# Up-projection of a decoder step: the four sums of weight blocks of a feature pair made by adding transfers instead of vector adds, their signs turned, and the weights fetched one more pair ahead

## The chip, the cores and the metric

The kernel runs on one core of a Trainium2 chip. The metric is the device time of one execution in microseconds, the median of several. A profile of one further execution gives the busy time of each engine and a trace of its instructions. The engines are TensorE (PE; its weight loads are listed as PEld), VectorE (DVE), ScalarE (ACT), GpSimd (POOL) and SyncE (SP), which only issues transfers. Each engine runs its own list of instructions in order. Transfers run on 16 DMA engines; SyncE, ScalarE and GpSimd issue them from their lists.

## The reference

One step of a decoder layer for 1024 prompt rows and 8 sequences of 4 sample rows, 1056 rows in all. The change lies in the feed-forward part:

```python
h2 = rmsnorm(x, g_norm2) * (1 + scale2) + shift2
up = h2 @ w_up                       # 1056 x 1024 by 1024 x 5632
prev = zeros if conv_prev is None else conv_prev
upc = concatenate([prev, up], axis=1)
conv = b_conv
for k in range(CONV_W):              # causal, depthwise, width 3
    conv = conv + w_conv[k] * upc[:, k:k + T]
a, gv = split(conv, 2, axis=-1)      # 2816 features each
x = x + gate2 * ((gelu(a) * gv) @ w_down)
```

Before it stand the norms, a gated chunk mixer, the attention with its page gathers, and `w_out`; behind it the final norm. All is float32.

## The kernel before

Features stand on the 128 partitions and rows run along the free dimension. `x1`, `hr` and the results are tiles of 128 x 1056 for 128 features each (R = 1056; HR = 528 is half of the rows; HB = 264 a quarter, which is what one PSUM bank takes in a matmul here). A float32 product is made in three matmuls per 128 x 128 block. Both operands are split into a leading part and a remainder (for weights by `parts`: ScalarE's cast L328, VectorE's subtraction L329), and the products leading x leading, leading x remainder and remainder x leading are summed in PSUM (L61).

The up-projection runs over 22 *pairs* of feature blocks: pair j makes block j of the `a` half (tile `ua`) and block 22 + j of the gate half (tile `ug`). It treats the product as a 2 x 2 block product: the weights of a pair are four blocks of 128 x 512, `a11`, `a12` (block j, input features 0 to 511 and 512 to 1023) and `a21`, `a22` (block 22 + j), and the activations four of 512 x 528. Seven products of blocks are then enough rather than eight. Four of them have sums of weight blocks as their weights:

```python
s1 = a21 + a22;  s2 = s1 - a11;  s3 = a11 - a21;  s4 = a12 - s2
```

and four have sums of activation blocks, `T1` to `T4`, which are made once. `F[k]`, `b1(k)`, `b2(k)` and `sums_of` are steps on the way to them, `turned` splits one of them into its two parts, and `B22` is the split block of the last activations. One `product` is 4 blocks of 128 inputs x 3 matmuls x 2 banks = 24 matmuls of 264 columns.

`pair_weights(j)` issues the loads of the four blocks on SyncE (`raw_load`, L1402, a ring of six tiles `raw`), loads the sample rows' convolution state `cst` (L1576), and makes the sums in two large tiles (`add_up`, L1582 to L1585), on GpSimd for every pair but the first and on VectorE for pair 0. It is called for pair j just ahead of `pair(j, ...)`. The large tiles come from `slot()`, a ring shared with the activation tiles, so a new pair waits until an old tile is free.

For pairs 0 to 3, `first_products` has the two products with `a11` and `a12` begun while the last rows of the activations are still in the making, between the steps of their norm: the squares of the last eighth (ScalarE L1463) are added (VectorE L1464), summed over the features on TensorE, and turned into scales. The other five products of these pairs follow later, in `pair`. In it VectorE adds the products into `ua` and `ug` (L1604, L1647), ScalarE copies (L1635), and `conv` makes the convolution of either half in three steps (ScalarE L1555, VectorE L1556 and L1557), with two small copies of the last rows on GpSimd (L1551, L1552). Then come gelu on ScalarE (L1660), the product of the halves on GpSimd (L1661, L1663), and the store of the result (L1664, GpSimd's queue). A new `up` tile begins with a memset on GpSimd (L1532) and the state rows (L1596).

The list of each engine is fixed when the program is built: a scheduler places the instructions of the program there, not always in the order of the source, and a position once given is kept whatever the chip then does.

## Time and profile before

| | |
|---|---|
| median of 3 runs | 1919.66 us (1917.22 to 1921.19) |
| the profiled execution | 1922.04 us, its span 1920.4 us |
| mean granted TensorE clock | 0.99 |
| first 264-column matmul of the up-projection | 1173.48 us |
| end of its last one | 1647.55 us |
| 264-column matmuls in between | 3696 |
| moved over the span | 345.09 MB, 180 GB/s |

Times in the trace are counted from the span's start. A row of the trace's course has the start, the duration, the engine, the line, the operation, the tiles written and read with their shapes, and the number of instructions in the row. In brackets stands how long the engine was idle before and what ended that. A group has its busy time, the mean duration of one in ns, and the idle time ahead of it with what ended most of it.

### The profile page before, as it was taken

What the parts mean: (1) busy time and instruction counts of PE and PEld (TensorE: products, weight loads), DVE (VectorE), ACT (ScalarE), POOL (GpSimd) and SP (SyncE); (2) the same over time, 40 slices, a digit from 0 to 9 for tenths busy, and PEclk for the clock granted to TensorE, in tenths of its full rate; (3) what the DMA queues carried; (4) which work ended last, traced back from release to release, by engine and by line L of the source; (5) the groups of instructions that cost most, each with busy time, mean ns of one, the idle gap of its engine ahead of it and who ended that gap; (6) DMA issues with size and microseconds to landing.
All of it is one profiled execution on the core that took longest, in us unless ns stands there. A gap on an engine that the chain in (4) does not pass through costs nothing.

```text
span 1920.4 us, 43666 instructions
## 1 busy us (share of the span) xinstructions
PE 1837.8 (96%) x16037; PEld 1728.4 (90%) x16037; DVE 1148.1 (60%) x2417; ACT 803.0 (42%) x1646; POOL 532.0 (28%) x741
## 2 busy tenths in 40 slices
PE   5799999999999999999999999989999999999997
PEld 3799999999998776867789998889999999999997
DVE  7714411111115667676666678998888888757464
ACT  4313111112115554655642367444444444555343
POOL 2410110000002122232202311667666665301010
PEclk9899999999999999999999999999999999999999
DMA  9454656767557778876854454233322223767463
GB/s 336 139 173 141 206 185 204 239 222 220 188 188 260 233 240 275 268 224 221 266 189 181 135 166 136 78 112 101 106 87 78 82 77 98 256 218 227 127 197 110
DMA packets 241319, 345.09 MB, mean 180 GB/s; under 512 B 35249, under 2 KB 172881, under 8 KB 238929
## 3 DMA queue, kind: packets, MB, share of 16 engines
q1 hardware_dynamic: 186976, 245.08, 39.8%
q0 software_dynamic: 17232, 56.00, 8.5%
q10 hardware_dynamic: 36896, 41.22, 6.9%
q8 instruction: 127, 2.08, 0.4%
q14 instruction: 88, 0.71, 0.1%
HBM read 304.91 MB, written 41.43 MB: 180 GB/s over the span
## 4 chain that ended last, share of the span: by engine, by line
PE 82%; DVE 7%; DMA 5%; ACT 3%; issue 2%; SPq 1%; POOL 1%; DVEq 0%; ACTq 0%; POOLq 0%
PE t L61 79%; PE t L65 3%; DMA t<-w_ada 2%; DVE t L329 1%; DMA t<-t 1%; DMA t<-psel 1%; DVE t L1556 1%; SPq L532 1%; ACT t L328 1%; ACT t L1145 1%; DMA t<-xT 1%; DVE t L1679 1%; DVE t L347 0%; DVE t L1557 0%; DVE t L1604 0%
## 5 line engine op out<-in xcount | busy, mean ns | idle before, releaser
L61 PE MATMUL t<-t,t 128*128 128x264 f32 (+14 forms) x15262 | 1763.8, 304 | 66.2 <-DVE t L182 14.9
L61 PEld LDWEIGHTS t<-t,t 128*128 128x128 f32 (+2 forms) x15102 | 1647.1, 169 | 124.4 <-issue 51.1
L329 DVE TENSOR_TENSOR t<-t,t 128x512 fp32r<-128x512 f32 (+2 forms) x478 | 386.0, 816 | 322.0 <-ACT t L328 316.7
L328 ACT CAST t<-t 128x512 fp32r<-128x512 f32 (+5 forms) x544 | 311.3, 589 | 410.0 <-PE t L61 281.0
L1604 DVE TENSOR_TENSOR t<-t,t 128x264 f32<-128x264 f32 (+2 forms) x296 | 92.1, 344 | 33.0 <-PE t L61 30.7
L65 PEld LDWEIGHTS t<-t,t 128*128 128x128 f32 x746 | 80.9, 143 | 32.3 <-issue 8.2
L65 PE MATMUL t<-t,t 128*128 128x128 f32 x746 | 106.4, 278 | 3.0 <-ACT t L1212 1.5
L532 POOL DMA_DIRECT2D t<-psel x128 | 70.3, 550 | 73.0 <-PE t L61 24.5
L693 ACT ACTIVATE t<-t 128x384 f32<-128x384 f32 (+1 forms) x48 | 22.2, 465 | 135.2 <-PE t L61 68.8
L1759 POOL TENSOR_TENSOR t<-t,t 128x384 f32<-128x384 f32 (+1 forms) x12 | 13.9, 1191 | 223.9 <-ACT t L1826 223.9
L695 POOL DMA_DIRECT2D t<-t x16 | 8.5, 531 | 241.6 <-DVE t L694 186.8
L1174 ACT COPY t<-t 128x512 f32<-128x512 f32 (+1 forms) x112 | 59.6, 569 | 35.4 <-PE t L65 35.2
L1556 DVE SCALAR_TENSOR_TENSOR t<-t,t,t 128x1072 f32<-128x1072 f32 x44 | 72.1, 1638 | 3.9 <-ACT t L1555 3.8
L1555 ACT ACTIVATE t<-t,t 128x1072 f32<-128x1072 f32 x44 | 56.6, 1286 | 41.3 <-DVE t L1604 27.1
L1144 DVE TENSOR_REDUCE t<-t 128x1 f32<-128x640 f32 (+3 forms) x64 | 58.7, 919 | 22.5 <-PE t L61 21.9
L1557 DVE SCALAR_TENSOR_TENSOR t<-t,t,t 128x1072 f32<-128x1072 f32 x44 | 69.5, 1581 | 0.0
L1145 ACT ACTIVATE t<-t,t 128x640 f32<-128x640 f32 (+3 forms) x64 | 56.3, 880 | 25.6 <-DVE t L1144 23.0
L1661 POOL TENSOR_TENSOR t<-t,t 128x1024 f32<-128x1024 f32 x22 | 53.2, 2417 | 21.7 <-ACT t L1660 21.7
L1201 POOL COPY t<-t 128x256 f32<-128x256 f32 x32 | 12.9, 402 | 124.1 <-DVE t L1199 61.5
L720 POOL TENSOR_TENSOR t<-t,t 128x512 f32<-128x512 f32 (+1 forms) x12 | 12.3, 1042 | 125.8 <-DVE t L711 97.8
L1582 POOL TENSOR_TENSOR t<-t,t 128x512 f32<-128x512 f32 x21 | 28.6, 1363 | 62.4 <-DVE t L1679 34.5
L1436 POOL TENSOR_TENSOR t<-t,t 128x384 f32<-128x384 f32 (+1 forms) x24 | 27.9, 1169 | 64.6 <-DVE t L1435 61.4
(274 smaller groups left out, 1253.5 us busy)
## 6 DMA issues: line engine op xcount, KB each, us to landing
t<-psel SPq DMA_DIRECT2D x384, 128.0 KB
t<-pcmp SPq DMA_DIRECT2D x332, 128.0 KB
t<-w_down SPq DMA_DIRECT2D x120, 256.0 KB
t<-t POOLq DMA_DIRECT2D x50, 528.0 KB, 4.1
t<-w_up SPq DMA_DIRECT2D x96, 256.0 KB
t<-pcmp ACTq DMA_DIRECT2D x180, 128.0 KB
t<-w_ada SPq DMA_DIRECT2D x16, 1024.0 KB
t<-psel POOLq DMA_DIRECT2D x128, 128.0 KB, 3.9
```

The lines of the kernel that those rows point to most:

```text
L61: return pe.matmul(out, lhsT, rhs, start=start, stop=stop, skip_group_check=skip)
L65: return pe.transpose(out, x, ident)
L328: act.copy(hi, t)
L329: dve.tensor_tensor(lo, t, hi.bitcast(F32), op=OP.subtract)
L532: d = queue.dma_start(dst, src[bass.ds(r, 1)].rearrange("g p c -> p (g c)"))
L1144: dve.tensor_reduce(m4[:, branch, h:h + 1], ps[:, :, 0:w], axis=AX.XY, op=OP.max, negate=True)
L1145: act.activation(P[:, 0:L].rearrange("p (a c) -> p a c", a=2), ps[:, :, 0:w], AF.Exp, bias=m4[:, branch, h:h + 1], accum_out=s4[:, branch, ...
L1174: (act.copy if w > 2 else dve.tensor_copy)(probs[branch, h][:, 128 * k:128 * (k + w)], pt[:, c:c + 128 * w])
L1555: act.activation(acc[:, 0:w], up[:, 0:w], AF.Identity, scale=cw[:, n, 0:1], bias=cw[:, n, 3:4])
L1556: dve.scalar_tensor_tensor(acc[:, 0:w], up[:, 1:1 + w], cw[:, n, 1:2], acc[:, 0:w], op0=OP.mult, op1=OP.add)
L1557: dve.scalar_tensor_tensor(acc[:, 0:w], up[:, 2:2 + w], cw[:, n, 2:3], acc[:, 0:w], op0=OP.mult, op1=OP.add)
L1604: dve.tensor_tensor(o, by4(banks[c][:, c0:c0 + n], n), other(c, c0, n), op=OP.add)
```

## The change

The sums are not added by an engine any more. `a21` is loaded straight into the place of `s1`. ScalarE writes -`a11` into the places of `s2` and `s3`, and -`a12` into that of `s4` (three instructions, L1586 of the changed kernel). Four transfers on GpSimd's queue then add while they write: `a21` into both `s2` and `s3` at once (L1587), `a22` into `s1` (L1588), `a22` into `s2` when the first has landed (L1590), and `s2` into `s4` when that has landed (L1592). So `s1` and `s2` are what they were, and `s3` and `s4` have the other sign. To match, `F[k]` has the other sign, and so has `T3`, which is made of it; `B22` is turned as well (`turned` with a sign, L1690 and L1691). These steps are a generator, `sums()`, that `pair` advances at five places (`next(ahead, None)`), and the weights of pair j + 1 are fetched ahead of `pair(j, ...)` rather than those of pair j.

```diff
     def pair_weights(j):
-        a11, a12, a21, a22 = (raw_load(A["w_up"][n][:, c:c + 512]) for n in (j, 22 + j) for c in (0, 512))
+        W1, W2 = A["w_up"][j], A["w_up"][22 + j]
+        a11, a12 = (raw_load(W1[:, c:c + 512]) for c in (0, 512))
+        t0, t1 = (R5B([128, RU], F32, "acc", 2) if j == 0 else slot() for _ in range(2))
+        s1, s4, s2 = t0[:, 0:512], t0[:, 512:1024], t1[:, 0:512]
+        s23 = t1[:, 0:1024].rearrange("p (s c) -> p s c", s=2)
+        sync.dma_start(s1, W2[:, 0:512])
+        a22 = raw_load(W2[:, 512:1024])
...
-        t0, t1 = (R5B([128, RU], F32, "acc", 2) if j == 0 else slot() for _ in range(2))
-        s1, s2, s3, s4 = t0[:, 0:512], t0[:, 512:1024], t1[:, 0:512], t1[:, 512:1024]
-        def add_up():
-            eng = pool if j else dve
-            eng.tensor_tensor(s1, a21, a22, op=OP.add)
-            eng.tensor_tensor(s2, s1, a11, op=OP.subtract)
-            eng.tensor_tensor(s3, a11, a21, op=OP.subtract)
-            eng.tensor_tensor(s4, a12, s2, op=OP.subtract)
-        if j:
-            add_up()
-        return cst, (a11, a12, a22), (s1, s2, s3, s4), add_up
+        def sums():
+            for o, x in ((s2, a11), (t1[:, 512:1024], a11), (s4, a12)):
+                act.activation(o, x, AF.Identity, scale=-1.0)
+            pool.dma_start(s23, W2[:, None, 0:512].to_broadcast([128, 2, 512]), accum_op=OP.add)
+            pool.dma_start(s1, W2[:, 512:1024], accum_op=OP.add)
+            yield
+            pool.dma_start(s2, W2[:, 512:1024], accum_op=OP.add)
+            yield
+            pool.dma_start(s4, s2, accum_op=OP.add)
+        return cst, (a11, a12, a22), (s1, s2, t1[:, 512:1024], s4), sums()
...
-    def turned(x, t):
+    def turned(x, t, sign=None):
+        hi = t[:, 0:HR].bitcast(F32)
+        if sign:
+            act.activation(t[:, 0:HR], x, AF.Identity, scale=sign)
+            dve.scalar_tensor_tensor(t[:, HR:R], x, sign, hi, op0=OP.mult, op1=OP.subtract)
+            return t
...
-        dve.tensor_tensor(F[k][0], b2(4 + k), b2(k), op=OP.subtract)
-        dve.tensor_tensor(F[k][1], F[k][0], b1(k), op=OP.add)
+        dve.tensor_tensor(F[k][0], b2(k), b2(4 + k), op=OP.subtract)
+        dve.tensor_tensor(F[k][1], b1(k), F[k][0], op=OP.subtract)
...
-        B22.append(turned(b2(4 + k), slot(F32R)))
+        B22.append(turned(b2(4 + k), slot(F32R), -1.0))
     for j in range(22):
-        if j:
-            loaded.append(pair_weights(j))
-        end = pair(j, *loaded[j], begun[j] if j < len(begun) else None)
+        ahead = iter(())
+        if j < 21:
+            loaded.append(pair_weights(j + 1))
+            ahead = loaded[j + 1][3]
+        end = pair(j, *loaded[j], begun[j] if j < len(begun) else None, ahead)
```

In `pair`, lines move down by 5 to 10: L1604 becomes L1609, L1635 L1642, L1647 L1655, L1660 L1670, L1661 L1671, L1664 L1674; L1678 and L1679 become L1693 and L1694, L1596 becomes L1601.

The change moves instructions at two places. The first is the opening of the stage. VectorE's list there, before the change, from the squares' additions on; t2123 and t2124 are the tiles of pair 0's sums, t1858 the last block of x, t2022 the sum of squares:

```order
L1464 TENSOR_TENSOR t2022_16010<-t2022_16010,t2076_16303 128x288
L1448 SCALAR_TENSOR_TENSOR t1858_15195<-t2083_16323,t61_262,t1858_15195 128x256
L1451 TENSOR_TENSOR t2084_16349<-t2083_16323,t61_262 128x32
L1582 TENSOR_TENSOR t2123_16439<-t2120_16432,t2121_16434 128x512
L1584 TENSOR_TENSOR t2124_16440<-t2118_16428,t2120_16432 128x512
L329 TENSOR_TENSOR t2102_16401<-t2100_16398,t2101_16400 128x512
L1453 TENSOR_TENSOR t1858_15195<-t1858_15195,t2084_16349 128x32
L1583 TENSOR_TENSOR t2123_16439<-t2123_16439,t2118_16428 128x512
L1464 TENSOR_TENSOR t2022_16010<-t2022_16010,t2085_16352 128x288
```

In the changed program ScalarE's list has, ahead of the squares L1463 that the last of these rows adds (t2120 and t2121 are now the tiles of the sums, t2118 and t2119 are `a11` and `a12`):

```order
L328 CAST t2098_16394<-t2097_16392 128x512
L1463 ACTIVATE t2076_16303<-t1857_15194 128x288
L328 CAST t2101_16400<-t2100_16398 128x512
L1586 ACTIVATE t2120_16432<-t2119_16430 128x512
L1586 ACTIVATE t2121_16433<-t2118_16428 128x512 x2
L1463 ACTIVATE t2085_16352<-t1858_15195 128x288
```

VectorE's four adds are gone from ahead of and behind L1453, and ScalarE's three L1586 stand between the cast and the last L1463, where nothing stood.

The second place is the passage from pair 0 to pair 1. ScalarE's list before the change (t2181 and t2182 are the convolution of the two halves of pair 0, t2188 and t2189 the sums of pair 1):

```order
L1678 CAST t2160_16786<-t1867_15220 128x528
L328 CAST t2196_17002<-t2188_16985 128x512
L328 CAST t2198_17033<-t2188_16985 128x512
L328 CAST t2200_17061<-t2189_16986 128x512
L1555 ACTIVATE t2181_16960<-t2162_16791,t2115_16424 128x1072
L328 CAST t2204_17097<-t2186_16980 128x512
L1555 ACTIVATE t2182_16966<-t2161_16789,t2115_16424 128x1072
```

and in the changed program, where t2186 and t2187 are that convolution, t2162 and t2163 the sums of pair 1, t2190 and t2191 those of pair 2, t2216 of pair 3:

```order
L1586 ACTIVATE t2162_16795<-t2161_16793 128x512
L1586 ACTIVATE t2163_16796<-t2160_16791 128x512 x2
L1586 ACTIVATE t2190_16999<-t2189_16997 128x512
L1586 ACTIVATE t2191_17000<-t2188_16995 128x512 x2
L1555 ACTIVATE t2186_16980<-t2167_16805,t2115_16424 128x1072
L1586 ACTIVATE t2216_17203<-t2215_17201 128x512
L1555 ACTIVATE t2187_16986<-t2166_16803,t2115_16424 128x1072
L1670 ACT_TABLE_LOAD
L1670 ACTIVATE t2187_16986<-t2187_16986 128x1072
L1642 COPY t2220_17211<-t2139_16608 128x528
L328 CAST t2200_17018<-t2163_16796 128x512
L328 CAST t2202_17054<-t2162_16795 128x512
```

Three casts of pair 1's sums stood ahead of pair 0's convolution; now the first of them (t2200) stands behind it, the gelu and a copy. GpSimd's list at the same place, in the changed program:

```order
L1588 DMA t2162_16795<-w_up 128x512
L1587 DMA t2163_16796<-w_up 128x2x512
L1587 DMA t2191_17000<-w_up 128x2x512
L1551 COPY t2116_16426<-t2167_16805 128x2
L1552 COPY t2116_16426<-t2167_16805 128x16
L1588 DMA t2190_16999<-w_up 128x512
L1590 DMA t2163_16796<-w_up 128x512
L1551 COPY t2116_16426<-t2166_16803 128x2
L1552 COPY t2116_16426<-t2166_16803 128x16
L1532 MEMSET t2195_17009 128x2
L1601 COPY t2195_17009<-t2165_16800 128x8x2
L1590 DMA t2191_17000<-w_up 128x512
```

Where this list had L1582 to L1585 for pair 1, it now issues the adding transfers of pairs 1 and 2, with the copies of pair 0's rows between them; L1590 for t2163 is the one whose result the cast t2200 reads. On TensorE the first matmul that reads t2200 stands right behind the last one of pair 0, while before the change matmuls of pair 1 stood between those of pair 0's last product.

More of the change, by code (lines that the diff above doesn't have):

```diff
@@ L1576, in pair_weights, with pair @@
             sync.dma_start(cst[:, i], A["st_cv"][:, 22 * i + j].rearrange("p b t -> p (b t)"))
-        t0, t1 = (R5B([128, RU], F32, "acc", 2) if j == 0 else slot() for _ in range(2))
-        s1, s2, s3, s4 = t0[:, 0:512], t0[:, 512:1024], t1[:, 0:512], t1[:, 512:1024]
-        def add_up():
-            eng = pool if j else dve
-            eng.tensor_tensor(s1, a21, a22, op=OP.add)
-            eng.tensor_tensor(s2, s1, a11, op=OP.subtract)
-            eng.tensor_tensor(s3, a11, a21, op=OP.subtract)
-            eng.tensor_tensor(s4, a12, s2, op=OP.subtract)
-        if j:
-            add_up()
-        return cst, (a11, a12, a22), (s1, s2, s3, s4), add_up
-    def pair(j, cst, raws, sums, add_up, begun=None):
+        def sums():
[8 more added lines that the diff above has]
+        return cst, (a11, a12, a22), (s1, s2, t1[:, 512:1024], s4), sums()
+    def pair(j, cst, raws, sums, _, begun, ahead):
         (a11, a12, a22), (s1, s2, s3, s4) = raws, sums
@@ L1620, in pair @@
             add(ua, 1, S, p1)
+            next(ahead, None)
             product(a12, BS[4:8], X, False)
@@ L1627, in pair @@
             add(ug, 1, Z, half_of(ug))
+            next(ahead, None)
             product(a22, T4, S, False)
@@ L1637, in pair @@
             add(ua, 1, S, p1)
+            next(ahead, None)
             if j:
@@ L1651, in pair @@
             add(ug, 1, Z, u3)
+            next(ahead, None)
             X = [pA(), pA()]
@@ L1659, in pair @@
         a = conv(j, ua)
+        next(ahead, None)
         act.activation(a[:, 0:RU - 2], a[:, 0:RU - 2], AF.Gelu_apprx_tanh)
@@ L1693, in step_kernel @@
     sums_of(0)
-    loaded[0][3]()
+    next(loaded[0][3])
     begun.append(first_products(1, [(0, m2), (0, m2), (0, m2)]))
     sums_of(1)
+    next(loaded[0][3])
     early.append(weights(A["w_up"][2], 8))
     sums_of(2)
+    next(loaded[0][3], None)
     begun.append(first_products(2))
```

2 lines of the change are left out of this document (1 added, 1 removed).

## Prediction

> **What bounds the kernel now.** I read the page first, then the stretches of the up-projection, then what TensorE waited for there.
>
> ```profile
> PE 1837.8 (96%) x16037; PEld 1728.4 (90%) x16037; DVE 1148.1 (60%) x2417; ACT 803.0 (42%) x1646; POOL 532.0 (28%) x741
> ...
> PE 82%; DVE 7%; DMA 5%; ACT 3%; issue 2%; SPq 1%; POOL 1%; DVEq 0%; ACTq 0%; POOLq 0%
> ```
>
> TensorE is busy for 96% of the span, and 82% of the chain that ended last is its own work. An edit on other engines can win only where TensorE stands still or runs at a lower clock. The next rows give, for stretches of the changed stage, their length, the busy time of TensorE, its weight loads, VectorE, ScalarE and GpSimd, the granted clock, the share of the DMA engines and GB/s; the last row is a wait of TensorE, with its total, its count and the longest.
>
> ```profile
> 1230.00:1280.00 50.00, 43.38 (x335) 42.43 (x334) 45.21 (x68) 18.90 (x24) 40.14 (x48) 0.97 0.35 111
> ...
> 1340.00:1360.00 20.00, 20.00 (x167) 20.00 (x166) 17.16 (x23) 8.64 (x14) 13.20 (x18) 1.00 0.30 93
> ...
> 1580.00:1630.00 50.00, 48.42 (x391) 47.61 (x391) 43.50 (x63) 23.87 (x38) 28.40 (x31) 1.00 0.30 94
> ...
> PE t L61 <- DVE t L1604: 10.2, 7, 3.3
> ```
>
> In the middle of the stage TensorE is busy 20.00 of 20.00 us, with 167 matmuls, 0.120 us each. A pair has seven products of 24 matmuls, 168 in all, so a pair takes 20.1 us and is bound by its matmuls. What the change takes off GpSimd there is worth nothing, though GpSimd works 13.20 of 20 us. Idle time is left at the two ends. At the front the last row counts seven waits for VectorE's L1604, 10.2 us together. At the end 50.00 − 48.42 = 1.6 us are missing.
>
> **The change, part by part.** First the opening, where the sums of pair 0 are made on VectorE now.
>
> ```profile
> 1173.54 0.62 ACT L328 CAST t<-t 128x512 fp32r<-128x512 f32 x1 [0.58 <-PE t L61]
> ...
> 1175.21 0.69 DVE L1582 TENSOR_TENSOR t<-t,t 128x512 f32<-128x512 f32 x1 [0.95 <-DMA t<-w_up]
> ...
> 1177.03 0.18 DVE L1453 TENSOR_TENSOR t<-t,t 128x32 f32<-128x32 f32 x1
> ...
> 1177.30 0.44 ACT L1463 ACTIVATE t<-t 128x288 f32<-128x288 f32 x1 [3.14 <-DVE t L1453]
> ...
> 1177.78 0.46 DVE L1464 TENSOR_TENSOR t<-t,t 128x288 f32<-128x288 f32 x1
> ...
> 1178.29 4.15 PE L61 MATMUL t<-t,t 128*128 128x1 f32 x18 [3.19 <-DVE t L1464]
> 1177.52:1184.34 6.82, 6.05 (x27) 5.62 (x28) 3.80 (x15) 1.39 (x5) 1.47 (x4) 0.50 0.56 180
> ```
>
> VectorE stands 0.95 us for a weight block, then runs two adds ahead of L1453, which ScalarE's L1463, VectorE's L1464 and TensorE's row sums need in turn. TensorE waits 3.19 us, and 6.82 us follow at half clock. The adds go. Three sign turns on ScalarE come ahead of L1463 instead; I price one as the 128x528 copy below, 0.62. ScalarE is free at 1173.54 + 0.62 = 1174.16; three turns end at 1176.0, L1463 at 1176.5, L1464 at 1176.9. The gap shrinks by **1.4 us** (0.8 if the weights land late, 1.9 if a turn costs the 0.44 of L1463) to 1.8. A gap of 2.99 us further on (below) brought no half clock, so 1.8 should not. Half clock for 6.05 us of busy time costs at most 3.0, but part of that is spent in a chain of short steps between engines; I take **1.7** (0 to 3.0).
>
> Next, the end of pair 0, where GpSimd makes the sums of pair 1.
>
> ```profile
> 1210.23 1.32 DVE L1679 TENSOR_TENSOR t<-t,t 128x528 fp32r<-128x528 f32 x2
> ...
> 1213.47 1.28 POOL L1582 TENSOR_TENSOR t<-t,t 128x512 f32<-128x512 f32 x1 [34.49 <-DVE t L1679]
> ...
> 1214.06 4.67 DVE L1679 TENSOR_TENSOR t<-t,t 128x528 fp32r<-128x528 f32 x3
> ...
> 1219.96 3.30 PE L61 MATMUL t<-t,t 128*128 128x264 f32 x25 [2.99 <-DVE t L1604]
> ...
> 1220.93 1.29 ACT L1555 ACTIVATE t<-t,t 128x1072 f32<-128x1072 f32 x1 [2.12 <-DVE t L1604]
> ```
>
> Alone, two of L1679 take 1.32 us, 0.66 each. Beside GpSimd's adds three take 4.67 instead of 2.0, so VectorE is 2.7 us late and TensorE waits 2.99. With no add on GpSimd this goes: **2.7** (2.4 to 3.0). The signed form that takes L1679's place for four tiles reads the same two operands of 128x528, so I price it alike; twice the elements in L1557 (below) cost 1.33, which agrees.
>
> Third, a **new wait**. The rows of the changed program put the casts of pair 1's first block, which must be complete, behind all of pair 0's convolution on ScalarE, and TensorE's first matmul of pair 1 behind the last product of pair 0 with nothing between. Today pair 1 fills that place.
>
> ```profile
> 1253.06 1.10 ACT L1660 ACTIVATE t<-t 128x1072 f32<-128x1072 f32 x1 [4.37 <-DVE t L1557]
> ...
> 1254.07 0.62 ACT L1635 COPY t<-t 128x528 f32<-128x528 f32 x1
> ...
> 1261.30 0.60 ACT L328 CAST t<-t 128x512 fp32r<-128x512 f32 x1
> 1261.42 1.33 DVE L1556 SCALAR_TENSOR_TENSOR t<-t,t,t 128x1072 f32<-128x1072 f32 x1 [0.47 <-ACT t L1555]
> 1262.68 0.49 DVE L1604 TENSOR_TENSOR t<-t,t 128x232 f32<-128x232 f32 x2
> ...
> 1263.68 1.33 DVE L1557 SCALAR_TENSOR_TENSOR t<-t,t,t 128x1072 f32<-128x1072 f32 x1
> ```
>
> Count from the start of that last product, 24 matmuls, over at 24 × 0.12 = 2.9 us. The first L1555 starts 1.0 later (1219.96 and 1220.93) and ends at 2.3. VectorE then runs L1556 to 3.6 and the last adds into the a half (0.49) to 4.1. The second L1555 ends at 5.4; L1557 of the first half runs beside it. L1556 and L1557 of the second half end at 8.05. Then gelu 1.10, the copy 0.62 and the cast 0.60 on ScalarE: 10.4. TensorE stands **7.5 us** (7 to 8.5). The copy also waits for a memset on GpSimd that stands behind two transfer issues, hence the upper end.
>
> Fourth, the clock behind that wait, and the waits that it replaces.
>
> ```profile
> 1245.65 5.59 PE L61 MATMUL t<-t,t 128*128 128x264 f32 x44 [0.70 <-DVE t L1604]
> ...
> 1253.30 4.60 DVE L329 TENSOR_TENSOR t<-t,t 128x512 fp32r<-128x512 f32 x1
> ...
> 1253.52 1.95 PE L61 MATMUL t<-t,t 128*128 128x264 f32 x14 [2.28 <-DVE t L1604]
> ...
> 1258.79 5.45 PE L61 MATMUL t<-t,t 128*128 128x264 f32 x30 [3.32 <-DVE t L1604]
> 1259.43:1262.85 3.42, 3.42 (x18) 3.42 (x17) 2.95 (x6) 1.79 (x2) 0.49 (x1) 0.50 0.43 162
> ```
>
> The gap of 3.19 was followed by 6.82 us at half clock, that of 3.32 by 3.42; the mean, 5.1, loses **2.6** (1.7 to 3.4). Against this, the waits for L1604 in pair 1 sum to 10.2 − 2.99 − 0.2 = 7.0, where 0.2 is the seventh wait, at the end of pair 0. They come from one place: convolution and casts of two pairs meet on VectorE, with adds on GpSimd beside them (one L329 lasted 4.60). After the new wait pair 0's convolution is over before pair 1 begins, so I take 6.5 of 7.0 as gone, with the 1.7 of that half clock: **8.2** (6 to 8.7).
>
> Fifth, the accumulating transfers. The trace of before has none. Their nearest rows are the plain ones that GpSimd issues.
>
> ```profile
> t<-t POOLq DMA_DIRECT2D x50, 528.0 KB, 4.1
> o_wsk<-wk POOLq DMA_DIRECT2D x8, 254.0 KB, 3.3
> o_k<-t POOLq DMA_DIRECT2D x2, 528.0 KB, 5.9
> L1664 POOL DMA_DIRECT2D t<-t x21 | 12.6, 599 | 8.4 <-POOL t L1663 5.1 <-issue 3.0 <-POOL t L1552 0.3
> ```
>
> Call X the landing of the one into two blocks (512 KB) and Y that of 256 KB. Plain, X + Y = 4.1 + 3.3 = 7.4. With both doubled it is 14.8, with 5.9 for X doubled 18.4. They are chained: L1590 waits for L1587, and the cast of s2 waits for L1590. For pair 1 the first is issued about when pair 0's last product starts, and ScalarE asks for the result 9.8 us later, so up to about 10 us are hidden by the convolution. The rows nearest in size and queue are 4.1 and 3.3; adding twice must not cost less than writing once, and I take 8 to 10, inside the cover. Without cover each us is one more us of the new wait: behind the waiting cast on ScalarE stand the other casts of pair 1, and TensorE needs all of them. Pairs 2 and later are asked for at least 20.1 us after, so they have room.
>
> Sixth, steady state. GpSimd loses 144.7 us of adds over 21 pairs (the sum of its four groups), 6.9 a pair, and gains four issues of 0.6:
>
> ```profile
> L1585 POOL TENSOR_TENSOR t<-t,t 128x512 f32<-128x512 f32 x21 | 42.0, 2002 | 1.3
> L1583 POOL TENSOR_TENSOR t<-t,t 128x512 f32<-128x512 f32 x21 | 41.3, 1968 | 0.1
> L1584 POOL TENSOR_TENSOR t<-t,t 128x512 f32<-128x512 f32 x21 | 32.8, 1561 | 0.0
> L1582 POOL TENSOR_TENSOR t<-t,t 128x512 f32<-128x512 f32 x21 | 28.6, 1363 | 62.4 <-DVE t L1679 34.5 <-DMA t<-w_up 27.9
> ```
>
> That makes 13.3 − 6.9 + 2.4 = 8.8 of 20.1 us busy. ScalarE goes from 8.7 to 10.5 with three turns. Loads by SyncE stay four a pair, and 1280 KB of accumulation are added, 65 GB/s on top of 93; 180 GB/s moved at a share of 0.56 in the opening. So TensorE stays the bound: **0**. At the end of the stage the adds of the last pairs go, which may give up to 1.6; I take **0.8**.
>
> Sum: −1.4 − 1.7 − 2.7 + 7.5 + 2.6 − 8.2 − 0.8 = **−4.7 us**. The profiled execution took 1922.04 (span 1920.4), so it would take 1917.3. The median of the runs is 2.4 lower; from 1919.66 the forecast is **1915.0**. With the ends of the terms not all on one side, its own range is 1911 to 1919.5. About 0.2%, 3.8 us, is what a measurement of this kernel can tell from no change, so the forecast is barely outside it.
>
> **The rivals.** *More gain*: no half clock follows the new wait and the whole tail closes, −4.7 − 2.6 − 0.8 = −8.1: 1911.6. The two rows at half clock behind gaps half as long speak against it.
>
> *Dear transfers*: X + Y = 14.8, each landing doubled. The cover of 10 is passed by 4.8 us, all of it in the new wait: 0.1 in sum, 1919.8. For it: an accumulation has to fetch the old value as well. Against it: the 528 KB landing is 0.8 us longer than the 254 KB one, so bytes are the smaller part of a landing.
>
> The Trainium skill, "Collectives: The Full Stack", in the part "Why ReduceScatter is half of AllGather" says that an add on the way costs a second source read, and so about half the rate (1.93 measured there). Taken as a factor on the whole landing this is the rival just told; taken on the bytes alone (0.8 us for 274 KB above) X is 5.5 and Y 4.1, an estimate of 9.6 that leaves the forecast as it is. No row of this trace decides between them.
>
> *Slower*: GpSimd runs in order, and both chained waits stand in its queue, ahead of the products L1671 and the copies that free tiles for the convolution. If nothing overlaps, a pair needs 8.8 + X + Y there, and passes 20.1 at X + Y = 11.3; with the 2.4 us product and the copies in between I put the deciding point at 14. Each us beyond it costs one in each of 18 pairs: at 16, 2 × 18 + 6 more in the new wait, about 1957. For it: the dearest of the three rows, 5.9, doubled for X and 3.3 doubled for Y make 18.4, past the point. Against it: the other row of that size is 4.1, and GpSimd's idle time grows from 6.8 to 11.3 us a pair, in which it can stand.
>
> **How the numbers follow.** Forecast 0.55 (0.35 of it faster by over 0.2%, 0.20 within), more gain 0.12 (faster), dear transfers 0.18 (0.15 within, 0.03 slower), slower 0.15. Faster 0.47, same 0.35, slower 0.18. The range 1909 to 1924 takes in the first three cases with the bounds of their terms and leaves most of the last out.
>
> **What would show it.** Row sums near 1176.9 and a full clock behind them; three L1691 or more at 0.7 in a row; one TensorE gap of 7 to 8 us where pair 1 starts, ended by ScalarE's L328, with half clock behind it; few gaps after; 20.00 of 20.00 in the middle. I am wrong if that gap ends on a transfer, if it is 12 us or more, or if gaps recur in every pair with GpSimd standing before L1590 or L1592.

## The result and the profile after

| | before | changed |
|---|---|---|
| median, four runs each on one chip | 1920.43 us (1917.22 to 1922.74) | 1944.16 us (1939.79 to 1945.03) |
| ratio of the medians, 95% interval | | 1.0123 (1.0107 to 1.0139) |
| the profiled execution, its span | 1922.04, 1920.4 us | 1939.79, 1938.2 us |
| first to last 264-column matmul | 474.07 us | 493.36 us |

The change costs 23.7 us; 1915.0 was forecast, with 1924 as the upper end. The profiled execution of the changed kernel was the lowest of its four, so its trace shows 17.8 us of the loss. All of that lies in the changed stage, which became 19.3 us longer. First the page of the changed kernel: its busy times, its chain, and the queue that GpSimd issues (packets, MB, share of 16 engines' span):

```profile
PE 1840.8 (95%) x16037; PEld 1731.1 (89%) x16037; DVE 1088.0 (56%) x2413; ACT 833.0 (43%) x1712; POOL 477.0 (25%) x745
...
q0 software_dynamic: 32720, 84.84, 17.3%
...
PE 81%; DMA 7%; DVE 5%; ACT 4%; issue 3%; POOL 1%; SPq 0%; DVEq 0%; ACTq 0%; POOLq 0%
```

VectorE and GpSimd became lighter, by 60 and 55 us, as planned. Transfers went from 5% to 7% of the chain. Next the waits of TensorE in the stage, from 1165 to 1680 us (total, count, longest):

```profile
PE t L61 <- ACT t L328: 10.8, 1, 10.8
PE t L61 <- ACT t L1623: 7.1, 8, 1.8
PE t L61 <- DVE t L1609: 6.6, 1, 6.6
PE t L61 <- ACT t L1586: 3.9, 1, 3.9
PE t L61 <- DVE t L1464: 1.5, 1, 1.5
```

Three long gaps at the front (10.8, 6.6, 3.9) and eight short ones in the middle (7.1 together). The stretches of the stage, first before the change and then after (length, then busy time and count of TensorE, weight loads, VectorE, ScalarE, GpSimd, then clock, DMA share, GB/s):

```profile
1165.00:1300.00 135.00, 121.81 (x943) 119.61 (x942) 122.62 (x218) 66.27 (x113) 70.91 (x85) 0.96 0.33 103
1300.00:1600.00 300.00, 299.51 (x2459) 298.97 (x2459) 257.76 (x368) 132.01 (x206) 205.69 (x233) 1.00 0.28 89
```

```profile
1165.00:1300.00 135.00, 109.19 (x824) 106.99 (x823) 91.37 (x191) 69.73 (x126) 72.52 (x84) 0.90 0.71 162
1300.00:1600.00 300.00, 294.54 (x2406) 292.89 (x2405) 216.75 (x362) 148.91 (x245) 145.78 (x229) 1.00 0.67 152
1595.00:1645.00 50.00, 50.00 (x411) 49.81 (x410) 38.78 (x69) 26.07 (x42) 19.41 (x30) 1.00 0.45 120
```

The counts of matmuls say where the loss is. In the first 135 us TensorE gets 119 fewer done, in the next 300 another 53; at 0.12 us each that is 14.3 and 6.4 us. Near the end of the stage, where 1.6 us were missing in a stretch of 50, TensorE is now busy 50.00. And the DMA share more than doubled.

**The front** has three places. The first is the end of pair 0 (start, duration, engine, line, in brackets the idle time before it and what ended it):

```profile
1182.59 23.89 POOL L1601 COPY t<-t 128x16 f32<-128x16 f32 x1
1206.41 0.86 POOL L1592 DMA_DIRECT2D t<-t  x1
...
1210.97 0.62 ACT L328 CAST t<-t 128x512 fp32r<-128x512 f32 x1 [6.51 <-DMA t<-t]
...
1212.58 3.21 ACT L1586 ACTIVATE t<-t 128x512 f32<-128x512 f32 x6
...
1214.78 5.62 PE L61 MATMUL t<-t,t 128*128 128x264 f32 x24 [3.93 <-ACT t L1586]
```

A copy of 128x16 elements on GpSimd, 0.52 us in the median, lasted 23.89. The transfer that completes `s4` of pair 0 stands behind it and is issued at 1206.41. ScalarE has stood 6.51 us for its landing when the cast starts, with six turns of later pairs queued behind, and TensorE loses 3.93. The second place is the start of pair 1:

```profile
1214.52 1.20 POOL L1587 DMA_DIRECT2D t<-w_up  x1 [3.44 <-DVE t L1655]
...
1224.52 0.86 POOL L1590 DMA_DIRECT2D t<-w_up  x1 [2.68 <-DMA t<-w_up]
...
1226.03 0.61 ACT L1642 COPY t<-t 128x528 f32<-128x528 f32 x1
1230.53 2.18 ACT L328 CAST t<-t 128x512 fp32r<-128x512 f32 x4 [3.89 <-issue]
...
1231.20 4.97 PE L61 MATMUL t<-t,t 128*128 128x264 f32 x28 [10.80 <-ACT t L328]
```

The first adding transfer is issued at 1214.52 and the second, which waits for it, at 1224.52: X = 10.0. The cast that needs the second starts at 1230.53: Y = 6.0. The row names no releaser for it, but by the trace that transfer has landed at 1230.46. ScalarE was free at 1226.64 and stands 3.89 us; TensorE waits 10.80. The third place is two pairs further on:

```profile
1266.20 0.91 POOL L1592 DMA_DIRECT2D t<-t  x1 [3.79 <-DMA t<-w_up]
1266.79 2.69 POOL L1671 TENSOR_TENSOR t<-t,t 128x1024 f32<-128x1024 f32 x1
...
1269.73 1.28 ACT L1555 ACTIVATE t<-t,t 128x1072 f32<-128x1072 f32 x1 [10.14 <-POOL t L1673]
...
1272.93 18.82 PE L61 MATMUL t<-t,t 128*128 128x264 f32 x132 [6.58 <-DVE t L1609]
```

GpSimd stands 3.79 us until a landing lets it go on, the product L1671 stands behind it, ScalarE's convolution waits for that product, VectorE for ScalarE, and TensorE loses 6.58.

**The middle** loses little at a time:

```profile
1413.95 0.33 SPq L1402 DMA_DIRECT2D t<-w_up  x1
...
1419.37 0.63 ACT L1586 ACTIVATE t<-t 128x512 f32<-128x512 f32 x1 [1.84 <-DMA t<-w_up]
1419.90 0.36 ACT L1623 COPY t<-t 128x264 f32<-128x264 f32 x1
...
1420.32 3.93 PE L61 MATMUL t<-t,t 128*128 128x264 f32 x30 [1.56 <-ACT t L1623]
```

A plain weight load of SyncE takes 5.4 us until ScalarE can turn the block. ScalarE stands 1.84 us for it, and the copy L1623, which needs none of this, stands behind the turn; TensorE needs that copy.

### The profile page after: what moved, and what is told of

Same layout as the page of the kernel before. It is cut to its first block, busy times and chain, and to the rows that moved or that the text cites. A ratio compares the mean times of both kernels' runs of the same rounds, so it can differ in the third digit from the quotient of the medians.

```text
span 1938.2 us, 43814 instructions
## 1 busy us (share of the span) xinstructions
PE 1840.8 (95%) x16037; PEld 1731.1 (89%) x16037; DVE 1088.0 (56%) x2413; ACT 833.0 (43%) x1712; POOL 477.0 (25%) x745
## 3 DMA queue, kind: packets, MB, share of 16 engines
q0 software_dynamic: 32720, 84.84, 17.3%
## 4 chain that ended last, share of the span: by engine, by line
PE 81%; DMA 7%; DVE 5%; ACT 4%; issue 3%; POOL 1%; SPq 0%; DVEq 0%; ACTq 0%; POOLq 0%
PE t L61 77%; PE t L65 3%; DMA t<-w_up 3%; DMA t<-w_ada 1%; DMA t<-t 1%; ACT t L328 1%; DMA t<-psel 1%; DVE t L329 1%; ACT t L1145 1%; DVE t L1694 0%; DMA t<-xT 0%; DVE t L347 0%; ACT t L1174 0%; DVE t L874 0%; ACT t L320 0%
## 5 line engine op out<-in xcount | busy, mean ns | idle before, releaser
L329 DVE TENSOR_TENSOR t<-t,t 128x512 fp32r<-128x512 f32 (+2 forms) x478 | 354.5, 750 | 376.6 <-ACT t L328 356.4
L1609 DVE TENSOR_TENSOR t<-t,t 128x264 f32<-128x264 f32 (+2 forms) x296 | 92.7, 347 | 41.3 <-PE t L61 40.2
L1586 ACT ACTIVATE t<-t 128x512 f32<-128x512 f32 x66 | 38.8, 624 | 77.7 <-DMA t<-w_up 73.4
L1778 POOL TENSOR_TENSOR t<-t,t 128x384 f32<-128x384 f32 (+1 forms) x12 | 13.9, 1192 | 225.0 <-ACT t L1845 225.0
L1556 DVE SCALAR_TENSOR_TENSOR t<-t,t,t 128x1072 f32<-128x1072 f32 x44 | 58.6, 1332 | 18.1 <-ACT t L1555 17.6
L1671 POOL TENSOR_TENSOR t<-t,t 128x1024 f32<-128x1024 f32 x22 | 58.5, 2660 | 10.7 <-ACT t L1670 10.7
L1557 DVE SCALAR_TENSOR_TENSOR t<-t,t,t 128x1072 f32<-128x1072 f32 x44 | 58.4, 1326 | 0.1
L1601 POOL COPY t<-t 128x16 f32<-128x16 f32 x44 | 45.4, 1050 | 0.0
L563 ACT ACTIVATE t<-t,t 128x128 f32<-128x128 f32 x16 | 7.9, 493 | 85.6 <-PE t L61 85.6
L1590 POOL DMA_DIRECT2D t<-w_up x22 | 19.4, 881 | 102.5 <-DMA t<-w_up 94.5
```

The source lines that it names most:

```text
L329: dve.tensor_tensor(lo, t, hi.bitcast(F32), op=OP.subtract)
L1556: dve.scalar_tensor_tensor(acc[:, 0:w], up[:, 1:1 + w], cw[:, n, 1:2], acc[:, 0:w], op0=OP.mult, op1=OP.add)
L1557: dve.scalar_tensor_tensor(acc[:, 0:w], up[:, 2:2 + w], cw[:, n, 2:3], acc[:, 0:w], op0=OP.mult, op1=OP.add)
L1609: dve.tensor_tensor(o, by4(banks[c][:, c0:c0 + n], n), other(c, c0, n), op=OP.add)
L1671: pool.tensor_tensor(a[:, 0:NP], a[:, 0:NP], g[:, 0:NP], op=OP.mult)
```

## The experiments

Seventeen kernels ran, each against the kernel before on the same chip. "Stage" is the time from the first to the last 264-column matmul in the profiled execution, 474.1 us before the change and 493.4 after it. "Front" and "middle" are the matmuls done from 1165 to 1300 and from 1300 to 1600 us; 943 and 2459 before the change, 824 and 2406 after it, 2470 when TensorE never stops. Up to e12 and from e15 on the stage began between 1169.4 and 1179.4 us (1173.5 before), so a front can differ by some 50 matmuls that are not the edit's. e2, e5 and e9 leave sums of weight blocks out.

| run | edit | median us | ratio (95%) | stage | front | middle |
|---|---|---|---|---|---|---|
| e1 | state copies on ScalarE | 1940.70 | 1.0104 (1.0076 to 1.0132) | 497.2 | 854 | 2355 |
| e2 | no transfer adds | 1919.36 | 0.9987 (0.9975 to 0.9998) | 472.9 | 922 | 2470 |
| e3 | sums by adds, one pair ahead | 1920.06 | 0.9994 (0.9981 to 1.0007) | 471.8 | 931 | 2470 |
| e4 | the same, all on VectorE | 1922.91 | 1.0012 (1.0001 to 1.0023) | 475.3 | 904 | 2470 |
| e5 | e1 and e2 together | 1917.25 | 0.9983 (0.9971 to 0.9995) | 471.8 | 938 | 2465 |
| e6 | third turn behind the gelu | 1956.54 | 1.0202 (1.0180 to 1.0224) | 508.6 | 853 | 2283 |
| e7 | product of the halves on VectorE | 1941.78 | 1.0111 (1.0094 to 1.0128) | 494.6 | 833 | 2379 |
| e8 | transfers for pair 0 alone, copies on ScalarE | 1921.14 | 1.0002 (0.9988 to 1.0016) | 471.2 | 931 | 2470 |
| e9 | one of the four transfers adds | 1941.12 | 1.0107 (1.0084 to 1.0130) | 485.4 | 877 | 2411 |
| e10 | window copies eleven pairs later | 1952.92 | 1.0168 (1.0151 to 1.0185) | 497.4 | 833 | 2393 |
| e11 | `s2` and `s3` added apart | 1978.23 | 1.0299 (1.0280 to 1.0319) | 530.2 | 870 | 2103 |
| e12 | transfers from pair 4 on | 1941.01 | 1.0115 (1.0090 to 1.0139) | 481.7 | 928 | 2393 |
| e13 | e3 and unused adding transfers | 2033.95 | 1.0583 (1.0546 to 1.0619) | 474.7 | | |
| e14 | e3 and unused plain transfers | 1984.72 | 1.0336 (1.0303 to 1.0370) | 470.6 | | |
| e15 | turns on GpSimd | 1944.64 | 1.0113 (1.0082 to 1.0144) | 497.5 | 743 | 2465 |
| e16 | e3 on GpSimd alone, copies on ScalarE | 1921.39 | 1.0005 (0.9990 to 1.0020) | 472.4 | 929 | 2470 |
| e17 | e12, turns on GpSimd | 1925.30 | 1.0022 (1.0007 to 1.0038) | 478.7 | 888 | 2462 |

### Is it the adding?

e2 takes the adding away, and the sums with it, and leaves every transfer, its size, its queue and its place:

```diff
-pool.dma_start(s1, W2[:, 512:1024], accum_op=OP.add)
+pool.dma_start(s1, W2[:, 512:1024])
```

and so for the other three.

> The changed kernel with the four transfers of a pair writing without adding, so the sums of weight blocks are left out and the result with them; sizes, queues, order and waits are the same. Theory B1 (adding itself makes a landing long, as it has to fetch the old value): the medians of 7.4 and 5.6 us fall to 4 to 5 and 3 to 3.5, and the time by 10 us or more, to 1925 to 1934. Rival B2 (the landing is long because of the queue, the load on the DMA engines or GpSimd's descriptors): the landings stay within 1 us and the time within 5 us of 1944.

The loss is gone: 1919.36, 0.13% below the kernel before. Its page and its stretches:

```profile
q0 software_dynamic: 25680, 84.84, 13.0%
```

```profile
1165.00:1300.00 135.00, 118.60 (x922) 116.66 (x922) 105.99 (x211) 76.23 (x134) 72.37 (x92) 0.95 0.56 179
1300.00:1600.00 300.00, 300.00 (x2470) 300.00 (x2470) 216.35 (x371) 158.04 (x254) 136.90 (x231) 1.00 0.46 153
```

The queue carries the same 84.84 MB. With adding it has 7040 packets more, one for each 4 KB of the 22 x 1280 KB that are added, and its packets take 17.3% of 1938.2 us instead of 13.0% of 1919.7: on 16 engines 5365 against 3993 us of engine time. At the plain mean of 47.1 us per MB the 28.8 MB would cost 1357; adding puts 1372 on top, a factor of 2.0. Among the packets of the trace, 7040 of 4 KB have become 14080 of 2 KB, and one of 2 KB takes as long (0.19 us) as one of 4 KB (0.20 in e2). In the middle the share is 0.67 against 0.46 at the same rate (152 and 153 GB/s). Landings from 1160 to 1680 us, of the changed kernel and then of e2 (KB each, median us):

```profile
t<-t POOLq DMA_DIRECT2D x24, 528.0 KB, 5.0
t<-w_up POOLq DMA_DIRECT2D x22, 512.0 KB, 7.4
t<-w_up POOLq DMA_DIRECT2D x44, 256.0 KB, 5.6
```

```profile
t<-t POOLq DMA_DIRECT2D x30, 528.0 KB, 3.9
t<-w_up POOLq DMA_DIRECT2D x22, 512.0 KB, 4.3
t<-w_up POOLq DMA_DIRECT2D x44, 256.0 KB, 4.0
```

The last row mixes two transfers: L1588, issued right behind L1587, lands in 7.5 us in the median (4.3 in e2), and L1590, issued when L1587 has landed, in 4.1 (2.9). The 528 KB rows are stores that add nothing, and they land later too; for the 22 stores L1674 alone the medians are 5.0 and 3.4. The waits of ScalarE for plain weight loads from 1300 to 1600 us are twice as long in the changed kernel as in e2:

```profile
ACT t L1586 <- DMA t<-w_up: 59.3, 28, 3.9
```

```profile
ACT t L1586 <- DMA t<-w_up: 28.0, 28, 1.7
```

By the landings in the trace, two thirds of the 59.3 are at the first turn of a pair, whose load lands no later after its issue than in e2 (2.8 us, 2.9 there). The load of the third turn is issued right behind L1587 and lands in 5.0 us in the median, 4.35 in e2; L1623, which TensorE needs, stands behind that turn.

The wait at pair 1 is 8.15 us in e2, and the copy on GpSimd is as long there (24.81) and costs 3.47. Plain transfers also shorten the issues on GpSimd (0.72 us for 1.23 at L1587); that this is not what the middle lacks is seen from e15 below, where GpSimd has more to do and the middle runs full.

### Is it the fetch one pair ahead, or the order?

e3 and e4 keep that fetch, the signs and the turned activations, and make the sums by adds again (e3 as here, e4 with `eng = dve`; e16 with `eng = pool` and e1's copies):

```diff
-pool.dma_start(s23, W2[:, None, 0:512].to_broadcast([128, 2, 512]), accum_op=OP.add)
...
+eng = pool if j else dve
+eng.tensor_tensor(t1[:, 512:1024], s1, a11, op=OP.subtract)
+eng.tensor_tensor(s1, s1, a22, op=OP.add)
+eng.tensor_tensor(s2, s1, a11, op=OP.subtract)
+eng.tensor_tensor(s4, s2, a12, op=OP.subtract)
```

> The changed kernel with the sums made again by four vector adds (GpSimd; VectorE for pair 0), one pair ahead and with the changed signs; a21 is still loaded straight into the place of s1, three loads into the ring per pair. Theory B (transfers are what costs): the time comes back to that of before, 1916 to 1924. Rival C (the order that comes with fetching one more pair ahead, which puts the casts of pair 1 behind the convolution of pair 0, costs most): a gap of 7 us or more at pair 1 stays, and the time is 1928 or more.

> As the run with GpSimd adds, but all four adds on VectorE for every pair (0.68 us each, 2.7 us of 20.1 per pair). Theory B with the reading of before (GpSimd's adds and VectorE slow each other): no slow adds, GpSimd nearly idle, gaps at pairs 0 and 1 under 5 us in all, and a time below before, 1908 to 1917. Rival C: the gap at pair 1 stays at 7 us or more and the time is within 4 us of the run with GpSimd adds. Rival D: VectorE becomes late in steady state (35 + 7 of 50 us busy does not suggest it), over 1925.

> A version without transfers: all four adds on GpSimd for every pair, pair 0 too, one pair ahead, and the state copies on ScalarE; nothing is left out. If VectorE's adds for pair 0 are what lengthens the opening (a gap of 4.2 us with half clock behind it in the run with VectorE's adds there): 1912 to 1917. Rival: GpSimd's adds slow VectorE in the opening by as much: 1918 to 1922.

All three are within 0.2% of the kernel before, so the gains that e4 and e16 were to bring did not come. In e3 and e16 no wait of TensorE for the pairs is longer than 3.0 us; e4 has one of 7.3, near 1280 us and not at pair 1. The fetch ahead and the signs cost and gain nothing that can be told.

### The starved copy

e1 moves it, and e5 does so with e2's plain transfers:

```diff
-pool.tensor_copy(u[:, 1026:RU]...
+act.copy(u[:, 1026:RU]...
```

> The changed kernel with the state copies (L1601) on ScalarE instead of GpSimd; nothing is left out. Theory A (a GpSimd copy that lasted 23.89 us held back the transfer into s4 of pair 0): that transfer is issued at about 1188 us instead of 1206, TensorE's gap of 3.9 us before the last product of pair 0 goes, the sums of pair 1 start some us earlier, and the time falls by 5 to 12 us, to 1932 to 1939. Rival B (the landings of the adding transfers are what costs, and the copy only fills time that would be waited anyway): the transfer into s4 is no more late, but the wait at pair 1 stays at 10 us or more and the time stays within 4 us of 1944.

> Transfers that write without adding (so the sums are left out, and the result with them) and the state copies on ScalarE. Theory A2 (a copy on GpSimd of over 20 us holds the s4 transfer of pair 0 back, whatever the transfers cost): the gap of 3.5 us before pair 0's last product, which the run with plain transfers still had, goes, and the time falls to 1912 to 1916, which is what the forecast had for cheap transfers. Rival: the gap moves to the passage to pair 1, whose wait grows from 8.2 to 11 us or more, and the time stays at 1918 to 1921.

In e1 the transfer for `s4` of pair 0 is issued at 1185.62 instead of 1206.41, and the gap of 3.93 is gone. The time moves by 3.5 us, less than the spread of the runs, and the wait at pair 1 stays (10.9), as the expectation's rival had it; waits in the middle grow (from 7.1 us in eight; waits of TensorE in e1):

```profile
PE t L61 <- ACT t L328: 12.2, 2, 10.9
PE t L61 <- ACT t L1623: 9.7, 9, 2.3
```

So the copy makes that gap, but what it costs in time can't be told from the noise: e2 and e5 lie 2.1 us apart, on two chips, and their ratios, 0.9987 and 0.9983, have overlapping intervals.

### What stands in between

e7 makes the product L1671, L1673 on VectorE. e6 puts the third turn and `s4`'s transfer behind the gelu:

```diff
-for o, x in ((s2, a11), (t1[:, 512:1024], a11), (s4, a12)):
-    act.activation(o, x, AF.Identity, scale=-1.0)
+for o in (s2, t1[:, 512:1024]):
+    act.activation(o, a11, AF.Identity, scale=-1.0)
...
+    queue.enter_context(tc.issue_after(gelus[-1].ins))
+    act.activation(s4, a12, AF.Identity, scale=-1.0)
```

> The changed kernel with the product of the two halves (L1671, L1673) on VectorE instead of GpSimd; nothing is left out. Theory G (the wait of 6.6 us at pair 2 comes because those products stand in GpSimd's list behind a transfer issue that waits for a landing): that gap falls under 2 us, and with it one stretch at half clock; the time falls by 6 to 12 us, to 1932 to 1938. Rival F2 (the tiles are late for other reasons): a gap of 5 us or more stays near 1266, and the time within 4 us of 1944.

> The changed kernel with the third sign turn of a pair (-a12 into s4, and the transfer that adds s2 to it) put behind the gelu of the pair ahead; nothing is left out. Theory E (in the middle of the stage ScalarE stands in its turn for a weight load that is late, and the copy L1623 that TensorE needs stands behind it): the waits for L1623, 7.1 us in eight, fall under 2 us, and the time by about 5 us, to 1937 to 1941. Rival F (GpSimd's queue is what is late in the middle): the gaps stay at 5 us or more, now ended by another line.

Neither helps. In e7 the gap of 6.58 comes back as two, 4.6 and 6.1. Ahead of the first ScalarE had stood 7.32 us for a store to land, ahead of the second 7.86 for a weight load (two rows of ScalarE in e7):

```profile
1283.04 1.28 ACT L1555 ACTIVATE t<-t,t 128x1072 f32<-128x1072 f32 x1 [7.32 <-DMA t<-t]
...
1296.56 1.15 ACT L1586 ACTIVATE t<-t 128x512 f32<-128x512 f32 x2 [7.86 <-DMA t<-w_up]
```

GpSimd's product is in neither chain any more; both waits are for transfers that land late. In e6 the waits for L1623 shrink from 7.1 to 0.5, and those for the casts grow, since `s4` is now late:

```profile
PE t L61 <- ACT t L328: 31.2, 13, 11.6
```

The place in the middle is confirmed; the wait only moves.

e15 takes the turns off ScalarE and leaves all else:

```diff
-act.activation(o, x, AF.Identity, scale=-1.0)
+pool.tensor_scalar(o, x, -1.0, 0.0, op0=OP.mult, op1=OP.add)
```

> The changed kernel with the three sign turns of a pair on GpSimd instead of ScalarE; nothing is left out. Theory E2 (in the middle the loss comes through ScalarE, which stands in its turn for a late weight load): waits for L1623 fall under 2 us in all, and the time falls to 1932 to 1938. Rival (GpSimd then stands for the same load, with the transfer issues and the products behind it): the waits move to the casts of the sums, and the time is 1942 or more.

The middle of e15:

```profile
1300.00:1600.00 300.00, 299.56 (x2465) 299.35 (x2464) 231.98 (x368) 134.89 (x208) 176.23 (x280) 1.00 0.68 155
```

The middle runs full at a DMA share of 0.68 (0.67 in the changed kernel), so there the adding transfers cost only as long as the turns stand on ScalarE. By the landings in the trace the edit does two things at once: ScalarE no longer stands for loads, and only 4 of 44 loads are issued within 2.5 us behind a `w_up` transfer of GpSimd (15 of 43 in the changed kernel), so fewer land late. No run parts the two. The waits for L1623 are down to 0.4, as expected of theory E2, but not the time: the front lost 81 matmuls more than in the changed kernel (743 and 824), with waits of 9.4 and 12.4 for the casts, and the total is the same.

### Where the parts sit

e8 leaves the adding transfers to pair 0 alone; e12 uses them from pair 4 on; e17 is e12 with e15's turns:

```diff
+if j < 4:
+    eng = pool if j else dve
+    eng.tensor_tensor(t1[:, 512:1024], s1, a11, op=OP.subtract)
...
+    return
```

> A version that takes what seemed good: pair 0's sums by adding transfers (the short opening), all other pairs' by GpSimd's vector adds one pair ahead, state copies on ScalarE; nothing is left out. If the opening is worth what the trace says (a gap of 4.2 us and a stretch at half clock in the run with GpSimd adds): 1912 to 1917, faster than before by 0.2 to 0.45%. Rival: the adding transfers of pair 0 land late, or GpSimd's adds slow VectorE as before: 1918 to 1924, no difference.

> Pairs 0 to 3 with vector adds (GpSimd; VectorE for pair 0) one pair ahead, pairs 4 to 21 with the adding transfers; nothing is left out. This parts the front from the middle. If the front holds the loss of the long gaps and the half clock, and the middle the 7.1 us of waits for L1623: 1925 to 1931. Rival K (without the jam at the front the middle has room, as the sums are then ready well ahead): 1919 to 1923. Rival L (the middle costs more than it seemed): over 1933.

> As the run with transfers from pair 4 on (1941 us), with the three sign turns of these pairs on GpSimd instead of ScalarE; nothing is left out. If the loss in the middle comes through ScalarE, which stands in its turn for a late weight load, and the loss at the front through the late landings there, neither is left: 1919 to 1926, within 6 us of the run with GpSimd adds throughout. Rival M (adding transfers cost more than these two ways, on stores or loads of other stages or in what the profiled run does not show): 1930 or more.

e8 costs nothing, and gains nothing of what it was to gain. e12 has a normal front and loses in the middle; e17 loses next to nothing in the middle, and 40 matmuls at the front against e12 (the middle of e12, then of e17):

```profile
1300.00:1600.00 300.00, 294.83 (x2393) 293.83 (x2392) 213.91 (x358) 149.84 (x245) 145.37 (x221) 0.99 0.67 151
```

```profile
1300.00:1600.00 300.00, 299.32 (x2462) 299.11 (x2461) 230.91 (x369) 136.56 (x211) 174.84 (x274) 1.00 0.67 153
```

From e12 to e17 the time falls by 15.7 us (1.0115 to 1.0022 by the ratios), to 5.2 above e3. The adding transfers are still there, 18 pairs of them. The profiled executions show 11.3 of the 15.7, and the stage itself only 3.0 (481.7 and 478.7): 69 matmuls are won in the middle, 40 lost at the front, and in e12's execution the stage began 6.2 us later. So two ways are seen: late landings at the front, where pair 1 has no room, and after it ScalarE standing for loads that the transfers delay. How much of the loss each carries stays open: no run has the second mended and the first not without the front growing worse (e15).

### How much adding is too much

e9 lets only the first transfer (512 of 1280 KB a pair) add. e11 splits it: `s2` first, 256 KB, and `s3` behind the second transfer, so that the chain to `s2` moves fewer bytes. e10 moves sixteen copies to the caches (`windows`, 254 KB each) from pairs 1 to 8 to pairs 12 to 19.

```diff
-pool.dma_start(s23, W2[:, None, 0:512].to_broadcast([128, 2, 512]), accum_op=OP.add)
+pool.dma_start(s2, W2[:, 0:512], accum_op=OP.add)
...
+pool.dma_start(t1[:, 512:1024], W2[:, 0:512], accum_op=OP.add)
```

> The changed kernel in which only the transfer into s2 and s3 (512 KB) adds; the other three write without adding, so their sums are left out. Adding bytes go from 1280 to 512 KB a pair. Theory H (adding occupies the DMA engines for longer per byte, and everything on them lands later): the loss shrinks with the bytes, of 25 us about 40% stay, 1927 to 1932, and the landing of the plain ones (into s1 and s2) comes to between 4.0 and 5.6 us. Rival I (each adding transfer has a fixed delay of its own): the plain ones land in 4.0 as in the run without adding, that into s2 and s3 still takes 7 or more.

> The changed kernel with the broadcast transfer split: a21 is added to s2 alone (256 KB), then a22 to s2, and a21 to s3 in a transfer of its own; nothing is left out, adding bytes are the same, one issue more. Rival J (the chain of landings decides): the first landing falls from 7.4 (10.0 at pair 1) to 5 to 6 us, the wait at pair 1 from 10.8 to 8 us or less, and the time by 3 to 8 us. Theory H (the load on the DMA engines decides): the sum of the landings in the middle falls little, and the time stays within 3 us.

> The changed kernel with the eight pairs of DRAM to DRAM copies of the window state (508 KB each, L1680 and L1681) issued in pairs 12 to 19 instead of 1 to 8; nothing is left out. Theory H: the DMA engines are 0.86 busy in pairs 1 to 3 and have less to move there, so the gap of 6.6 us shrinks by 2 us or more, and the time falls by 3 to 6 us, while the middle of the stage loses a little. Rival J (the chain of landings decides, not the load): within 2 us of the changed kernel.

With 40% of the added bytes e9's queue has 2816 packets more than e2's, 40% of 7040, and its packets take 14.5% of 1937.2 us on 16 engines, 4494: just over a third of the 1372 on top. The loss is not in proportion. 1941.12 is nearly the whole, where 1927 to 1932 was expected. L1588, plain here and issued right behind the adding L1587, lands in 7.0 us, almost as late as in the changed kernel; L1590, issued when L1587 has landed, in 3.0, as in e2. (The median of the two together, 3.9, hides this.) ScalarE's turns stand for plain loads from 1300 to 1600 us as long as in the changed kernel (e9):

```profile
ACT t L1586 <- DMA t<-w_up: 60.8, 29, 3.5
```

The load of the third turn lands in 5.1 us. So one adding transfer of 512 KB a pair is enough. What counts is what is on the way beside it, and not the added bytes or the engine time in all. e11 is the worst. Its middle, 2103 matmuls, has this (the longest wait of TensorE in sum, then the course of one pair):

```profile
PE t L61 <- ACT t L1624: 28.7, 13, 5.2
```

```profile
1470.64 0.33 SPq L1402 DMA_DIRECT2D t<-w_up  x1
...
1478.24 0.63 ACT L1586 ACTIVATE t<-t 128x512 f32<-128x512 f32 x1 [6.65 <-DMA t<-w_up]
```

The same bytes in one more transfer: 256 KB adds land in 6.5 us, a plain load takes 7.6, and the wait at pair 1 is 11.1, no shorter than before. So fewer bytes ahead did not help, and one transfer more hurt; neither side of the expectation foresaw that. e10 was expected to relieve the front and got worse (13.4 us at pair 1, ahead of any copy that was moved); I have no explanation for it.

e13 and e14 add four more transfers a pair to e3, into memory that nobody reads, adding in e13 and plain in e14:

```diff
+if j:
+    pool.dma_start(idle_d[j], W2[:, None, 0:512].to_broadcast([128, 2, 512]), accum_op=OP.add)
+    pool.dma_start(idle_e[j][:, 0], W2[:, 512:1024], accum_op=OP.add)
```

and two more in the same way.

> The run with GpSimd adds one pair ahead (1920 us), with the four adding transfers of each pair but the first issued besides, into scratch in DRAM that nobody reads, 1280 KB a pair; nothing is left out. Theory H (adding transfers hold the DMA engines, and other transfers land late): weight loads and stores land late as in the changed kernel, waits of TensorE recur in the middle of the stage, and the time is 1926 or more, 5 us or more above the same run with plain transfers. Rival J (only waiting for their own landings costs): within 3 us of the run with plain ones.

> The same with the four extra transfers writing plainly; nothing is left out. Both theories: 1919 to 1924, the issues cost GpSimd 2.2 us a pair that it has. If this too is 1926 or more, it is the issues or the bytes and not the adding.

Both expectations missed, because three of the four need nothing but `w_up`: they were issued in the first 143 us, where the kernel waits for its loads. That made another measurement of it, for adding into DRAM. The stage begins at 1239.46 us in e14 and 1285.23 in e13, against 1173.48 before, so 22.0 MB there cost 66.0 us plain and 111.8 adding, a factor of 1.69.

## Why the prediction was wrong

**The opening: right.** The gap is 1.51 us (1.8 forecast), and the clock behind it is full:

```profile
1173.50:1180.00 6.50, 6.46 (x50) 6.11 (x51) 4.52 (x17) 3.20 (x8) 2.44 (x4) 1.00 0.97 247
```

**The end of pair 0: the contention went, a new stall came.** VectorE's steps run at 0.66 each again, as forecast:

```profile
1212.23 1.32 DVE L1691 SCALAR_TENSOR_TENSOR t<-t,t 128x528 fp32r<-128x528 f32 x2
```

The 2.99 us were not gained, though, since `s4`'s transfer stood behind the starved copy: 3.93 in their place.

**The new wait: the place and the sum right, the cover too small.** With plain transfers it is 8.15 us, at the place named (7.5 forecast, 7 to 8.5). With adding it is 10.80, because X + Y was 16.0 and ScalarE had asked 12.1 us after the issue; the 3.9 beyond that are the stand in ScalarE's row. The prediction took 8 to 10. This is its rival *dear transfers*, with 16.0 for that rival's 14.8; but that rival too asked only for the landing, and its 1919.8 is nearly as far off as the forecast.

**Half clock: mis-sized.** It was priced for one gap, 5.1 us long at a loss of 2.6. Three stretches of the changed kernel are granted half the clock, with the three gaps:

```profile
1213.60:1220.43 6.83, 5.62 (x24) 5.34 (x24) 3.79 (x10) 4.10 (x7) 2.72 (x4) 0.50 0.74 182
1223.90:1234.14 10.24, 2.94 (x13) 2.94 (x14) 3.59 (x5) 3.80 (x6) 5.46 (x12) 0.50 1.01 190
1268.20:1278.44 10.24, 5.51 (x25) 5.54 (x26) 5.82 (x10) 4.10 (x5) 6.59 (x14) 0.50 0.82 179
```

TensorE is busy 14.1 us in them, so at most half of that, 7.0, is lost where 2.6 was forecast.

**The waits of pair 1: gone where forecast, with another in their place.** The waits for the adds of pair 1 are down to one, but that one is 6.58, and it comes by the way that the rival *slower* named: GpSimd in order, a landing waited for ahead of L1671. Its deciding point, X + Y = 14, is passed at pair 1 (16.0) and not in the median, 7.4 for L1587 and 4.1 for L1590, 11.5. So GpSimd's list shows in TensorE's waits at one place, not in 18 pairs, and e7, which takes the product off it, loses as much.

**The fifth step failed**: it priced adding by the landing of the transfer itself, took X + Y as 8 to 10 (measured 11.5 in the median and 16.0 at pair 1; 7.2 plain in e2), and asked only whether that fits under the cover. **The sixth failed for the same reason**: "TensorE stays the bound: 0" counted the bytes, 65 GB/s on top of 93, and found room for them. Measured, adding transfers from pair 4 on cost 20.6 us by themselves (e12 against the kernel before). Beside an adding transfer the plain loads and stores land late too, and engines that run in order stand for them ahead of work that TensorE needs. e2 shows the cause (adding alone). e15 and e17 show that the loss in the middle goes when the turns leave ScalarE, where they stand 59.3 us for loads in 300 (28.0 in e2). Why the others land late is argued and not shown: adding takes twice the engine time of a plain transfer on engines that all share, but e9 loses nearly as much with a third of that extra time. The prediction weighed ScalarE by its busy time (8.7 to 10.5 of 20 us) and not by what its turns wait for. None of the rivals had this.

**The tail: right**, the 1.6 us are gone there against 0.8 forecast.

With plain transfers, where these two steps are taken out, the kernel stands 1.6 us below the one before (e2) and 2.9 with the copy moved (e5, 0.9983); both leave the sums out. The −4.7 forecast was too much even so, for e2 keeps 3.47 us of the copy's stall and 13.65 us at half clock. Of the versions that make the sums, none beats the kernel before: e3, e8 and e16 are level with it.

What stays open: e10; how one adding transfer makes the others late (e9, e11); the shares of the front and the middle; and part of the times, since the profiled execution lies 4.4 to 6.5 us below the median for the changed kernel, e10 and e12, though not for e1, e7 and e15.

## What to carry over

Price a transfer that adds by what it delays for all others on the way, and not by its own landing alone: one such transfer in four was enough for nearly the whole loss here. Then go through each in-order list for instructions that stand for a plain load, with work of the bound engine behind them. A transfer with twice the slack it needs can still cost time. To test such a change, keep every transfer and take only its arithmetic away: that run alone separated the order, which was harmless, from the adding.
